# The pooling stage of a two-layer encoder: scale folded into the map's weights, gate row finished earlier, boundary work reordered

## The chip, the cores and the metric

The kernel runs on one core of one Trainium2 chip. The metric is the time of one execution in microseconds (us), as the median of several runs. The core's engines run side by side, each through its own queue in order: TensorE (PE, its weight loads are PEld), VectorE (DVE), ScalarE (ACT), GpSimd (POOL), and SyncE (SP), which issues the loads from memory.

## The reference

The input is 256 tokens of 1024 channels. Two layers follow each other, each made of three sublayers: a SwiGLU with 2816 hidden channels, a token mixer, and a second SwiGLU. The mixer of layer 0 is a pooling mixer, that of layer 1 latent attention. Every sublayer is wrapped in the same way, with shift, scale and gate computed from a conditioning vector `c`:

```
h = rmsnorm(x, g_pre) * (1 + scale) + shift
y = rmsnorm(fn(h), g_post)
x = x + weight * (1 + gate) * y
```

The pooling mixer works in four groups of 256 channels. Group g takes the mean over a window of 2, 4, 8 or 16 tokens minus the token itself, multiplies by its 256x256 map, adds a bias and multiplies by a scale for every channel:

```
y = einsum('bsgc,gcd->bsgd', pooled - hg, w) + b
return y.reshape(B, S, D_MODEL) * scale
```

## The kernel before, in words

The 256 tokens are two token tiles of 128. A sublayer's input `h` lies turned (channels on partitions) as two float32r parts, hTH (the rounded value) and hTL (the rest), and every weight likewise: ACT casts a raw tile to the high part (line 263), VectorE subtracts it from the raw tile for the low part (line 271). A product is three matmuls, high by high, high by low, low by high (lines 98 to 100).

**Order of the work.** The program is recorded in the order in which the code calls it (no scheduler moves anything), so each engine runs its share in that order. The class `Bulk` holds one queue of all loads of the program: four raw buffers of 1 MB (`N_RAW`), each load followed by its ACT work and its VectorE work. A load is issued by SP when a raw buffer is free again, so VectorE's progress sets when loads start. `until`, `high`, `low_part` and `soft` let the stages run pieces of this queue at chosen places.

**A SwiGLU** (class `FFN`; f0 and f2 are those of layer 0) runs over 11 chunks of 256 hidden channels. `unit` does one chunk of one token tile: product with `wi`, silu and gate product `g` (lines 708, 710), transposes of `g` (724) with its split gH, gL (94, 95), product with `wo` into four accumulator banks (747). `head` does chunks 0 and 1 while tile 1's boundary work (`chain1`) is still under way; `tail` does chunks 9 and 10, tile 0 ahead of tile 1, so that tile 0's boundary is covered by tile 1's products.

**A boundary** from one sublayer to the next is a chain across engines, per token tile: sums of squares of y on ACT (508), `ms` on VectorE (501), the power on POOL (503), x += y * G * r on VectorE (535), sums of squares of x (ACT), `ms`, POOL, xr = x * r in halves on ACT and VectorE (554, 555), transposes on TensorE (562), modulation in halves on ACT and VectorE (576, 582), cast to hTH (588, 590) and hTL (593).

**Modulation vectors** take four 1 MB pieces of `ada_w` each (tiles `ada`), summed on VectorE over the conditioning channels into `aacc` (350, 352); TensorE then sums over partitions, either by eight matmuls of one column (361, `finish_cols`), by transposes that VectorE adds up (391 and 397, `finish_turned`), or, for a gate, into a row G on all partitions (448, then 456 and 457 add the bias and multiply by (1 + gate) g_post).

**The pooling stage** follows f0's tail. Tokens are mixed after the map, by a 256x256 matrix for each group. `pool_map` multiplies h of one tile by the map's parts pwH, pwL into z; ACT copies z out (1461, 1476, 1477); `pool_bias` starts an accumulator bank with the bias (954); `pool_mix` adds the mixed z (965); `pool_scale_rows` multiplies by the scale on VectorE into `pooly` (979), from which the boundary reads. The gate row of the pooling sublayer is reduced in the stage itself (448, 456, 457), and so are shift and scale of the next sublayer, vectors 6 and 7 (361). `warm` matmuls (108) keep TensorE occupied near the stage's end.

## Time and profile before

| | |
|---|---|
| median of 3 runs (lowest to highest) | 930.23 us (930.08 to 932.29) |
| profiled execution, span from first to last instruction | 928.2 us |
| its own time, with what lies around the span | not listed apart; 930.2 by the median of the runs, 2.0 beyond the span |
| TensorE busy | 902.1 us (97%) |
| TensorE weight loads | 741.1 us (80%) |
| VectorE busy | 705.8 us (76%) |
| ScalarE busy | 441.1 us (48%) |
| GpSimd busy | 41.9 us (5%) |
| read from memory | 233.51 MB, 253 GB/s over the span |

A timeline row reads: start in us from the span's first instruction, duration in us, engine, line of the kernel, operation, output <- inputs, shapes, how many instructions the row merges, and in brackets how long the engine had stood idle before it and what ended that. A windows row gives a stretch, its length, then for PE, PEld, DVE, ACT and POOL the busy time and the number of instructions, then the granted TensorE clock (1.00 is full), the DMA engines' busy share and the GB/s moved.

### The profile page before, as it was taken

What the parts mean: (1) busy time and instruction counts of PE and PEld (TensorE: products, weight loads), DVE (VectorE), ACT (ScalarE), POOL (GpSimd) and SP (SyncE); (2) the same over time, 40 slices, a digit from 0 to 9 for tenths busy, and PEclk for the clock granted to TensorE, in tenths of its full rate; (3) what the DMA queues carried; (4) which work ended last, traced back from release to release, by engine and by line L of the source; (5) the groups of instructions that cost most, each with busy time, mean ns of one, the idle gap of its engine ahead of it and who ended that gap; (6) DMA issues with size and microseconds to landing.
All of it is one profiled execution on the core that took longest, in us unless ns stands there. A gap on an engine that the chain in (4) does not pass through costs nothing.

```text
span 928.2 us, 11193 instructions
## 1 busy us (share of the span) xinstructions
PE 902.1 (97%) x4251; PEld 741.1 (80%) x4251; DVE 705.8 (76%) x856; ACT 441.1 (48%) x661; POOL 41.9 (5%) x56
## 2 busy tenths in 40 slices
...
GB/s 324 370 313 352 364 372 311 345 373 210 137 181 287 376 342 323 303 365 268 137 203 371 320 350 322 346 234 32 53 130 100 173 156 278 292 194 259 226 1 45
DMA packets 135973, 235.28 MB, mean 253 GB/s; under 512 B 5628, under 2 KB 98415, under 8 KB 135664
## 3 DMA queue, kind: packets, MB, share of 16 engines
...
q14 instruction: 20, 0.16, 0.0%
HBM read 233.51 MB, written 1.05 MB: 253 GB/s over the span
## 4 chain that ended last, share of the span: by engine, by line
PE 89%; DVE 4%; ACT 3%; issue 2%; DMA 1%; POOL 0%; SPq 0%; DVEq 0%; POOLq 0%; ACTq 0%
PE acc L747 25%; PE in L100 16%; PE in L98 16%; PE in L99 16%; PE accm L1314 2%; PE ps_g L724 2%; PE ps_h L562 1%; PE ps_mod L361 1%; DVE aacc L352 1%; PE in L794 1%; PE accp L965 1%; DMA adah<-in_ada_w_dram 1%; ACT p L1228 1%; DMA wi<-in_ffn_w_in_dram 1%; PE ps_turn L391 1%
## 5 line engine op out<-in xcount | busy, mean ns | idle before, releaser
L352 DVE SCALAR_TENSOR_TENSOR aacc<-ada,sc,aacc 128x1024 f32<-128x1024 f32 (+1 forms) x113 | 143.8, 1273 | 11.3 <-DMA ada<-in_ada_w_dram 9.1
L708 ACT ACTIVATE sil<-in 128x256 f32<-128x256 f32 x84 | 32.2, 383 | 247.7 <-PE in L100 240.4
L710 DVE TENSOR_TENSOR g<-in,sil 128x256 f32<-128x256 f32 x84 | 35.2, 420 | 52.4 <-ACT sil L708 52.3
L95 DVE TENSOR_TENSOR gL<-ps_g,gH 128x256 fp32r<-128x256 f32 x88 | 36.7, 417 | 23.6 <-ACT gH L94 23.5
L94 ACT CAST gH<-ps_g 128x256 fp32r<-128x256 f32 x88 | 32.4, 368 | 45.1 <-PE ps_g L724 45.0
L503 POOL TENSOR_TENSOR r<-ms,mhalf 128x1 f32<-128x1 f32 x24 | 13.6, 565 | 838.4 <-DVE ms L501 838.4
L724 PEld LDWEIGHTS ps_g<-ident,g 128*128 128x128 f32 x176 | 24.7, 140 | 11.5
L724 PE MATMUL ps_g<-ident,g 128*128 128x128 f32 x176 | 33.6, 272 | 0.0
L508 ACT ACTIVATE junk<-x 128x512 bf16<-128x512 f32 x24 | 15.1, 631 | 21.4 <-DVE x L535 11.3
L361 PE MATMUL ps_mod<-ones,aacc 128*128 128x1 f32 x96 | 12.7, 259 | 10.1 <-DVE cols L150 9.9
L576 ACT ACTIVATE hs<-ps_h,mod,mod 128x128 f32<-128x128 f32 x48 | 18.1, 458 | 8.4 <-DVE mod L377 5.0
L361 PEld LDWEIGHTS ps_mod<-ones,aacc 128*128 128x128 f32 x96 | 13.0, 210 | 11.2 <-DVE cols L150 10.1
L352 DVE SCALAR_TENSOR_TENSOR aacc<-adah,sc,aacc 128x512 f32<-128x512 f32 x28 | 21.0, 752 | 0.9
L582 DVE TENSOR_SCALAR hs<-ps_h,mod,mod 128x128 f32<-128x128 f32 x48 | 16.4, 404 | 5.2 <-PE ps_h L562 4.9
L535 DVE SCALAR_TENSOR_TENSOR x<-tmp,r,x 128x512 f32<-128x512 f32 x23 | 16.3, 749 | 2.2 <-POOL r L503 1.2
L1238 POOL TENSOR_SCALAR p<-p,rs 128x256 f32<-128x256 f32 x16 | 16.1, 1008 | 28.6 <-ACT p L1228 15.3
L554 ACT ACTIVATE xr<-x,r 128x512 f32<-128x512 f32 x12 | 8.7, 722 | 17.4 <-POOL r L503 17.4
L1228 ACT ACTIVATE p<-s,nm 128x256 f32<-128x256 f32 x32 | 14.9, 471 | 3.1 <-DVE nm L1220 2.6
L593 DVE TENSOR_TENSOR hTL<-hs,hTH 128x512 fp32r<-128x512 f32 x24 | 15.6, 688 | 0.4
L562 PE MATMUL ps_h<-ident,xr 128*128 128x128 f32 x96 | 14.3, 292 | 0.5 <-ACT xr L554 0.3
L271 DVE TENSOR_TENSOR wo10L<-wo,wo10H 128x2048 fp32r<-128x2048 f32 x4 | 9.2, 2293 | 7.4 <-ACT wo10H L263 7.4
L1263 PE MATMUL att<-pT,v 128*128 128x256 f32 x52 | 13.8, 389 | 0.5 <-ACT pT L1255 0.3
...
## 6 DMA issues: line engine op xcount, KB each, us to landing
...
```

The lines of the kernel that those rows point to most:

```text
L94: nc.scalar.copy(h, src)
L95: nc.vector.tensor_sub(lo, src, h.bitcast(F32))
L98: nc.tensor.matmul(ps, lhsT=lh, rhs=rh, start=first, stop=False)
L99: nc.tensor.matmul(ps, lhsT=lh, rhs=rl, start=False, stop=False)
L100: nc.tensor.matmul(ps, lhsT=ll, rhs=rh, start=False, stop=last)
L352: nc.vector.scalar_tensor_tensor(acc, w, sc[:, k : k + 1], acc, op0=ALU.mult, op1=ALU.add)
L361: nc.tensor.matmul(ps[:, j : j + 1], lhsT=acc[:, (j - j0) * P : (j - j0 + 1) * P], rhs=ones[:, 0:1], start=True, stop=True,)
L708: nc.scalar.activation(sil, ps[:, 0:CW], AF.Silu)
L710: nc.vector.tensor_mul(g, ps[:, CW : 2 * CW], sil)
L724: nc.tensor.transpose(ps[:, a * P : (a + 1) * P], g[:, a * P : (a + 1) * P], ident)
L747: nc.tensor.matmul(acc[hf], lhsT=lhs[:, a, :], rhs=rhs[:, a, hf * 512 : (hf + 1) * 512], start=f, stop=l)
L1228: nc.scalar.activation(p[:, t * S : (t + 1) * S], ps[:, t * S : (t + 1) * S], AF.Exp, bias=nm[:, t : t + 1], accum_out=sm[:, t : t + 1],)
```

## The change

1. The pooling scale is multiplied into the raw map `pw` on VectorE (`pool_scaled`, two halves) before it is split, and into the bias row (one partition, 1024 elements). The accumulator then holds the scaled result, and `pool_scale_rows` and `pooly` go.
2. The map, the scale row and the bias row are loaded earlier, together with the second of the four pieces of vector 7 (`with_pool`); until the map has been split, the queue of loads keeps three raw buffers instead of four (`limit`).
3. The gate row of the pooling sublayer is finished in f0's last chunks, in the place of its own sum `aacc` (`in_place`). Vector 6 is no longer held for the stage: it is turned in f0's body (`finish_turned`).
4. In the stage the boundary chain comes first on every engine: ACT's copies of z, the bias and mixing matmuls and the low parts of f2's first weights come after the chain's steps. The halves of xr and of the modulation change engines (`act_half`, `own`): the half that VectorE scales is also cast by VectorE.
5. f2's first low parts are cut into halves or quarters (`low_part`) and put at chosen places; all of wi01L and wi10L now stands behind the boundary's last VectorE instruction.
6. Matmuls on the low part hTL come last in `pool_map` and in the first half of chunk 0 in `head` (`low_last`; in f2, f3 and f5). Most `warm` matmuls go.

```diff
@@ class Bulk @@
+            self.limit = N_RAW
...
-                if out >= N_RAW:
+                if out >= self.limit:
@@ gate(..., in_place=False) @@
-                if hf == 0:
+                if hf == 0 and in_place:
+                    mods[layer, m] = acc
+                    st.append(acc)
+                elif hf == 0:
                     st.append(row_tile())
@@ mod_half(..., own=False) @@
-            if on_act:
+            if on_act != own:
                 nc.vector.tensor_copy(hh[:, bsl, :], hv)
@@ FFN.mm_in(..., low_last=False) @@
+            if low_last:
+                todo = [(hh, i, k) for k in ks for i in range(2)] + [(hl, 0, k) for k in ks]
...
@@ pooling mixer @@
+    def pool_load():
+        raw = raw_tile("pw")
+        nc.sync.dma_start(
+            raw.rearrange("p (k n) -> p k n", n=GW), pool_w[0].rearrange("g (a p) n -> p (g a) n", p=P)
+        )
+        sr = rowp.tile([P, D], F32, tag="xr", name="poolsc")
+        nc.sync.dma_start(sr, pool_scale[0:1, :].to_broadcast([P, D]))
+        br = rowp.tile([P, D], F32, tag="xr", name="poolb")
+        nc.sync.dma_start(br[0:1, :], pool_b[0:1].rearrange("l g n -> l (g n)"))
+        pool_st.update(raw=raw, sr=sr, br=br)
...
+    def pool_scaled(hf):
+        rv = pool_st["raw"][:, hf * 1024 : (hf + 1) * 1024].rearrange("p (g a n) -> p g a n", g=2, a=2)
+        sv = pool_st["sr"][:, hf * 512 : (hf + 1) * 512].rearrange("p (g n) -> p g n", g=2)
+        nc.vector.tensor_mul(rv, rv, sv.unsqueeze(2).to_broadcast([P, 2, 2, GW]))
...
-        nc.sync.dma_start(bs[0:1, 0:D], pool_b[0:1].rearrange("l g n -> l (g n)"))
-        nc.sync.dma_start(bs[:, D : 2 * D], pool_scale[0:1, :].to_broadcast([P, D]))
+        nc.vector.tensor_mul(bs[0:1, 0:D], pool_st["br"][0:1, :], pool_st["sr"][0:1, :])
@@ the program's loads @@
-    ss2 = shift_scale(0, 2, (6, 7))
+    ss2 = shift_scale(0, 2, (7,))
+    def with_pool():
+        bulk.limit = N_RAW - 1
+        pool_load()
+        ss2[5][1]()
+
+    early = (ss2[5][0], with_pool, *ss2[5][2:])
...
     def to_pool():
-        bulk.until(("pw",))
+        for hf in range(2):
+            a = hf * 1024
+            pool_scaled(hf)
+            bulk.high_part(("pw",), a, a + 1024)
+        bulk.low_part(("pw",), 0, 1024, False)
+        bulk.limit = N_RAW
+        bulk.low_part(("pw",), 1024, 2048, True)
+        pool_consts()
@@ layer 0, pooling (now) @@
+    s2 = post_add(1, acc1, r, mods[0, 2])
+    nc.scalar.copy(*z0[1])
...
+    xr = pre_scale(1, rstd(s2, 1.0), 1)
...
+    pool_mix(accp0, 0, 0)
...
+    pool_mix(accp0, 0, 1)
+    accp1 = acc_tile(1, "accp1")
+    pool_bias(1, accp1, 0)
+    after = reduce_held(0, 7, psum.tile([P, 512], F32, tag="in", name="ps_mod07"))
+    pool_bias(1, accp1, 1)
+    pool_mix(accp1, 1, 0)
+    G = mods[0, 5]
+    r = post_norm(0, accp0, 1.0, G)
...
+    h0()
+    h1()
+    l0()
+    l1()
+    bulk.low_part(wi(0, 1), 0, 1024, False)
+    bulk.low_part(wi(0, 1), 1024, 2048, True)
+    f2.high_in(1, 0)
+    bulk.low_part(wi(1, 0), 0, 1024, False)
+    bulk.low_part(wi(1, 0), 1024, 2048, True)
```

The first place where instructions move is VectorE's queue in f0's last chunks, between the last pieces of vector 7 and the boundary of tile 0 (`gL` is the low part of a turned chunk, `tmp` the boundary's first product). Before:

```order
L352 SCALAR_TENSOR_TENSOR aacc_1514<-ada_1454,sc,aacc_1514 128x1024 x2
L271 TENSOR_TENSOR wo10L<-wo_1458,wo10H 128x2048
L95 TENSOR_TENSOR gL_1582<-ps_g_1578,gH_1581 128x256
L710 TENSOR_TENSOR g_1587<-in_1542,sil_1585 128x256
L271 TENSOR_TENSOR pwL<-pw,pwH 128x2048
L95 TENSOR_TENSOR gL_1624<-ps_g_1620,gH_1623 128x256
L523 TENSOR_TENSOR tmp_1652<-acc_0_492,G_1145 128x512
```

The same place now:

```order
L457 TENSOR_TENSOR aacc_1327<-ps_row_1558,bc 128x512
L458 SCALAR_TENSOR_TENSOR aacc_1327<-aacc_1327,bc 128x512
L353 SCALAR_TENSOR_TENSOR aacc_1532<-ada_1474,sc,aacc_1532 128x1024 x2
L272 TENSOR_TENSOR wo10L<-wo_1505,wo10H 128x2048
L95 TENSOR_TENSOR gL_1601<-ps_g_1597,gH_1600 128x256
L721 TENSOR_TENSOR g_1606<-in_1562,sil_1604 128x256
L457 TENSOR_TENSOR aacc_1327<-ps_row_1608,bc 128x512
L458 SCALAR_TENSOR_TENSOR aacc_1327<-aacc_1327,bc 128x512
L944 TENSOR_TENSOR pw<-pw,poolsc 128x1024 x2
L272 TENSOR_TENSOR pwL<-pw,pwH 128x1024 x2
L950 TENSOR_TENSOR poolbs<-poolb,poolsc 1x1024
L95 TENSOR_TENSOR gL_1658<-ps_g_1654,gH_1657 128x256
```

Four gate instructions, two products with the scale row and the bias product now stand ahead of `gL` and so of the whole boundary of tile 0.

The second place is SP's queue of loads in the same chunks (`wo` is the last chunk's output weight, used by TensorE ahead of everything in the stage). Before:

```order
L291 DMA ada_1448<-in_ada_w_dram 128x2x1024
L291 DMA ada_1454<-in_ada_w_dram 128x2x1024
L657 DMA wo_1458<-in_ffn_w_out_dram 128x2x1024
L914 DMA pw<-in_pool_w_dram 128x8x256
L291 DMA ada_1517<-in_ada_w_dram 128x2x1024
```

The same place now:

```order
L292 DMA ada_1462<-in_ada_w_dram 128x2x1024
L923 DMA pw<-in_pool_w_dram 128x8x256
L927 DMA poolsc<-in_pool_scale_dram 128x1024
L929 DMA poolb<-in_pool_b_dram 1x1024
L292 DMA ada_1474<-in_ada_w_dram 128x2x1024
L662 DMA wo_1505<-in_ffn_w_out_dram 128x2x1024
L292 DMA ada_1589<-in_ada_w_dram 128x2x1024
```

The map (1 MB) and the scale row on all partitions (0.5 MB) moved ahead of the last `wo`.

The third place is VectorE's queue where f2 begins (`hTH` and `hTL` are f2's input for tile 0, `tmp` begins the boundary of tile 1). Before:

```order
L588 CAST hTH_1979<-hs_1986 128x512
L593 TENSOR_TENSOR hTL_1980<-hs_1986,hTH_1979 128x512
L593 TENSOR_TENSOR hTL_1980<-hs_1996,hTH_1979 128x512
L271 TENSOR_TENSOR wi10L<-wi_1704,wi10H 128x2048
L523 TENSOR_TENSOR tmp_2041<-pooly,G_1800 128x512
L501 SCALAR_TENSOR_TENSOR ms<-ss 128x1
L526 TENSOR_TENSOR tmp_2041<-pooly,G_1800 128x512
L535 SCALAR_TENSOR_TENSOR x_81<-tmp_2041,r,x_81 128x512 x2
L271 TENSOR_TENSOR wi11L<-wi_1882,wi11H 128x2048
```

The same place now:

```order
L593 CAST hTH_1964<-hs_1971 128x512
L598 TENSOR_TENSOR hTL_1965<-hs_1971,hTH_1964 128x512
L598 TENSOR_TENSOR hTL_1965<-hs_1981,hTH_1964 128x512
L272 TENSOR_TENSOR wi01L<-wi_1647,wi01H 128x1024 x2
L272 TENSOR_TENSOR wi10L<-wi_1733,wi10H 128x1024 x2
L527 TENSOR_TENSOR tmp_2034<-accp_0_1909,aacc_1327 128x512
L505 SCALAR_TENSOR_TENSOR ms<-ss 128x1
L530 TENSOR_TENSOR tmp_2034<-accp_1_1910,aacc_1327 128x512
L539 SCALAR_TENSOR_TENSOR x_81<-tmp_2034,r,x_81 128x512 x2
L272 TENSOR_TENSOR wi11L<-wi_1900,wi11H 128x2048
```

The low part wi01L, which was made ahead of the boundary of tile 0, now stands between f2's input and everything else.

## Rows read from the trace of the kernel before

**Rows 1.** Windows: the last chunks of f0, the pooling stage, f2's head.
```profile
204.00:211.00 7.00, 7.00 (x35) 5.75 (x33) 5.03 (x4) 2.45 (x3) 0.00 (x0) 1.00 0.98 360
...
222.87:252.89 30.02, 29.39 (x171) 24.01 (x169) 24.34 (x44) 19.74 (x39) 2.20 (x4) 0.94 0.37 130
252.89:264.74 11.85, 11.85 (x50) 9.05 (x51) 10.68 (x14) 6.33 (x9) 1.41 (x2) 1.00 0.44 131
264.74:300.00 35.26, 35.26 (x164) 29.23 (x164) 25.41 (x28) 17.19 (x22) 0.00 (x0) 1.00 0.74 246
```

**Rows 2.** Timeline of f0's last two chunks: ScalarE, VectorE and TensorE.
```profile
201.84 1.91 ACT L263 CAST wo10H<-wo 128x2048 fp32r<-128x2048 f32 x1 [4.29 <-DMA wo<-in_ffn_w_out_dram]
203.78 2.29 DVE L271 TENSOR_TENSOR wo10L<-wo,wo10H 128x2048 fp32r<-128x2048 f32 x1
...
211.62 0.42 DVE L95 TENSOR_TENSOR gL<-ps_g,gH 128x256 fp32r<-128x256 f32 x1 [1.30 <-ACT gH L94]
217.10 0.42 DVE L710 TENSOR_TENSOR g<-in,sil 128x256 f32<-128x256 f32 x1 [0.73 <-ACT sil L708]
217.62 0.38 PEld L724 LDWEIGHTS ps_g<-ident,g 128*128 128x128 f32 x2
...
222.87 0.19 PEld L98 LDWEIGHTS z<-pwH,hTH 128*128 128x128 f32 x1
```

**Rows 3.** Timeline of TensorE in f0's body, around four transposes and a gate's half row.
```profile
121.19 0.60 PE L391 MATMUL ps_turn<-ident,aacc 128*128 128x128 f32 x4
...
121.86 0.40 PE L99 MATMUL in<-wi50L,hTH 128*128 128x512 f32 x1
...
156.69 1.02 PE L448 MATMUL ps_row<-aacc,ones 128*128 128x512 f32 x2
...
157.78 0.40 PE L99 MATMUL in<-wi70L,hTH 128*128 128x512 f32 x1
```

**Rows 4.** One line of the gate row, and a half low part in the timeline.
```profile
L456 DVE TENSOR_TENSOR G<-ps_row,bc x10: 680/692/692, 148.5 to 882.7; 128x512 f32<-128x512 f32 x10
...
261.95 1.22 DVE L271 TENSOR_TENSOR wo0L<-wo,wo0H 128x1024 fp32r<-128x1024 f32 x1
```

**Rows 5.** Timeline of the pooling stage: the chain's places, both token tiles.
```profile
224.90 1.41 DVE L535 SCALAR_TENSOR_TENSOR x<-tmp,r,x 128x512 f32<-128x512 f32 x2
...
226.16 0.59 ACT L1461 COPY poolz<-z 128x512 f32<-128x512 f32 x1 [0.85 <-PE z L100]
...
229.17 0.72 ACT L554 ACTIVATE xr<-x,r 128x512 f32<-128x512 f32 x1 [1.05 <-POOL r L503]
...
231.59 1.04 PE L562 MATMUL ps_h<-ident,xr 128*128 128x128 f32 x8
...
234.47 0.19 PEld L98 LDWEIGHTS z<-pwH,hTH 128*128 128x128 f32 x1 [0.76 <-DVE hTH L588]
...
241.22 1.28 DVE L979 TENSOR_TENSOR pooly<-accp,poolbs 128x512 f32<-128x512 f32 x2
...
243.50 0.16 DVE L501 SCALAR_TENSOR_TENSOR ms<-ss 128x1 f32<-128x1 f32 x1 [0.41 <-ACT junk L508]
...
248.21 0.72 ACT L554 ACTIVATE xr<-x,r 128x512 f32<-128x512 f32 x1 [0.85 <-POOL r L503]
```

**Rows 6.** The clock near the stage's end: two windows, and twelve equal weight loads twice.
```profile
247.00:248.00 1.00, 1.00 (x6) 1.00 (x6) 0.30 (x2) 0.36 (x2) 0.37 (x1) 0.50 0.13 53
...
250.00:251.00 1.00, 1.00 (x10) 1.00 (x9) 0.00 (x0) 0.60 (x3) 0.00 (x0) 0.84 0.00 0
...
247.03 2.68 PEld L108 LDWEIGHTS warm<-ident 128*128 128x128 f32 x12
...
250.82 1.42 PEld L108 LDWEIGHTS warm<-ident 128*128 128x128 f32 x12
```

**Rows 7.** Timeline of f2's head: low part of chunk 1 and the end of tile 1's boundary.
```profile
261.75 0.19 PEld L99 LDWEIGHTS in<-wi11L,hTH 128*128 128x128 f32 x1 [0.34 <-DVE wi11L L271]
...
264.74 0.86 PEld L562 LDWEIGHTS ps_h<-ident,xr 128*128 128x128 f32 x8 [0.22 <-ACT xr L554]
```

More of the change, by code (lines that the diff above doesn't have):

```diff
@@ L550, in pre_xr, with pre_scale @@
         return pre_scale(t, rstd(s2, 1.0))
-    def pre_scale(t, r):
+    def pre_scale(t, r, act_half=0):
         xr = rowp.tile([P, D], F32, tag="xr", name=f"xr{t}")
-        nc.scalar.activation(xr[:, 0:512], xt[t][:, 0:512], AF.Copy, scale=r)
-        nc.vector.tensor_scalar(xr[:, 512:1024], xt[t][:, 512:1024], r, None, op0=ALU.mult)
+        a, v = (slice(hf * 512, (hf + 1) * 512) for hf in (act_half, 1 - act_half))
+        nc.scalar.activation(xr[:, a], xt[t][:, a], AF.Copy, scale=r)
+        nc.vector.tensor_scalar(xr[:, v], xt[t][:, v], r, None, op0=ALU.mult)
         return xr
@@ L698, in need_out, with mm_in @@
             bulk.until(("wo", self.layer, self.fi, c))
-        def mm_in(self, ps, c, t, hT, ks):
+        def mm_in(self, ps, c, t, hT, ks, low_last=False):
             hh, hl = hT
+            if low_last:
+                todo = [(hh, i, k) for k in ks for i in range(2)] + [(hl, 0, k) for k in ks]
+                for n, (lhs, i, k) in enumerate(todo):
+                    rhs = self.wi[c, k // 4][i][:, k % 4, :]
+                    nc.tensor.matmul(ps, lhsT=lhs[:, k, :], rhs=rhs, start=n == 0 and k == 0, stop=False)
+                return
             for k in ks:
@@ L711, in act, with inn @@
             self.st[c, t] = g
-        def inn(self, c, t, hT, mid=nop):
+        def inn(self, c, t, hT, mid=nop, low_last=False):
             ps = psum.tile([P, 512], F32, tag="in", name=f"in{c}{t}")
-            self.mm_in(ps, c, t, hT, range(4))
+            self.mm_in(ps, c, t, hT, range(4), low_last)
             mid()
@@ L754, in head @@
             self.need_in(0, 1)
-            ps = self.inn(0, 0, hT0)
+            ps = self.inn(0, 0, hT0, low_last=True)
             self.need_in(1, 0)
@@ L971, in pool_mix @@
             )
-    def pool_scale_rows(t, acc, halves=(0, 1)):
-        if "y" not in pool_st:
-            pool_st["y"] = hl_tile("pooly", F32)
-        y = pool_st["y"][:, t * D : (t + 1) * D]
-        for hf in halves:
-            sl = slice(hf * 512, (hf + 1) * 512)
-            nc.vector.tensor_mul(y[:, sl], acc[hf], pool_st["bs"][:, D + hf * 512 : D + (hf + 1) * 512])
-        return [y[:, 0:512], y[:, 512:1024]]
     mla = {}
@@ L1450 @@
     hT0 = ffn_tail(
         f0, hT, 0, 0, 0, 1, to_pool,
-        between=lambda: bulk.low_part(ada2, 0, 1, False),
-        between2=(lambda: bulk.low_part(ada2, 1, 2, False, 0, 512), last_ada2),
+        between=first_ada2,
+        between2=(lambda: bulk.low_part(ada2, 1, 2, False, 0, 512), lambda: bulk.low_part(ada2, 1, 2, True, 512, D)),
     )
     acc1 = f0.acc[1]
-    z0 = pool_map(0, hT0)
+    wi = lambda c, q: ("wi", 0, 1, c, q)
+    z0 = [pool_map(0, hT0, hf) for hf in range(2)]
     r = post_norm(1, acc1, 0.5, mods[0, 2])
-    for dst, src in z0:
-        nc.scalar.copy(dst, src)
@@ L1462 @@
-    s2 = post_add(1, acc1, r, mods[0, 2])
-    rows_of_gate = held["pool"]([psum.tile([P, 512], F32, tag="in", name=f"ps_row{hf}") for hf in range(2)])
-    rows_of_gate([0])
-    accp0 = pool_bias(0)
-    pool_mix(accp0, 0, 0)
-    xr = pre_xr(1, s2)
-    rows_of_gate([1])
-    bulk.low_part(ada3, 0, 1, False)
-    f2.high_in(0, 0)
-    hT1 = pre(1, xr, 0, 1)
-    accp1 = pool_bias(1)
-    (dst0, src0), (dst1, src1) = pool_map(1, hT1)
-    bulk.low_part(ada3, 1, 2, True)
-    f2.high_in(0, 1)
@@ L1493 @@
-    xr = pre_xr(0, s2)
-    pool_scale_rows(1, accp1, (1,))
-    ss = post_sq(y1, 1.0)
-    for f in after:
-        f()
-    hT0 = pre(0, xr, 0, 2)
-    more(6)
+    nc.scalar.copy(*z0[0])
+    s2 = post_add(1, acc1, r, mods[0, 2])
+    nc.scalar.copy(*z0[1])
+    accp0 = acc_tile(0, "accp0")
+    for hf in range(2):
+        pool_bias(0, accp0, hf)
+    xr = pre_scale(1, rstd(s2, 1.0), 1)
+    hT1 = new_hT(1)
+    h0, l0, _ = mod_half(1, 0, turn_half(1, 0, xr), hT1, 0, 1, False, True)
+    h1, l1, _ = mod_half(1, 1, turn_half(1, 1, xr), hT1, 0, 1, True, True)
@@ new lines @@
+    h0()
+    h1()
+    pool_mix(accp0, 0, 0)
+    l0()
+    bulk.low_part(ada3, 0, 1, False)
+    l1()
+    f2.high_in(0, 0)
+    z1 = [pool_map(1, hT1, hf) for hf in range(2)]
+    for dst, src in z1:
+        nc.scalar.copy(dst, src)
+    bulk.low_part(ada3, 1, 2, True)
+    bulk.low_part(wi(0, 0), 0, 1024, False)
+    pool_mix(accp0, 0, 1)
[3 more added lines that the diff above has]
+    pool_bias(1, accp1, 1)
```

98 lines of the change are left out of this document (43 added, 55 removed).

## The prediction

> **What bounds the kernel now.** I read the busy times by window first. TensorE is busy all the time in f0's last chunks, in f2's head and after it, and its clock is full there [rows 1]. So each matmul added to those stretches costs its own time, and whatever makes TensorE wait in the pooling stage is never made up later. The stage takes 30.0 us, most of it for waits along the boundary chains of the two token tiles. Second I read the timeline of f0's last chunks: VectorE works at 5.0 of 7.0 us there, idle mostly for ScalarE's casts (1.30 before gL), and the last `wo` comes late from memory (ScalarE idle 4.29 us for it) [rows 1, 2]. Third the timeline of the stage, for the places of the chain [rows 5], and fourth f2's head, where TensorE already waits 0.34 us for the low part wi11L and 0.22 us for the boundary of tile 1 [rows 7]: VectorE has no slack left there.
>
> The profiled span is 928.2 us and the median 930.2, so I put 2.0 us around the span and make the sum on 930.2.
>
> **First stretch, f0's body and tail.** TensorE gets eight transposes for vector 6, in two groups of four. From the start of such a group to the second matmul behind it are 0.67 us, where one matmul alone takes 0.23: 0.44 us each. The gate's half row costs 1.09 - 0.23 = 0.86 us [rows 3]. Together 2 x 0.44 + 2 x 0.86 = 2.6 us, all on the path, since TensorE has no gap here.
>
> VectorE gets more, and what decides is when it reaches `g` of the last chunk, for which TensorE comes at 217.62 before [rows 2] and at 220.2 with the 2.6 us. The last `wo` landed at 201.8 [rows 2]; 1.57 MB (map and scale row) now stand ahead of it in the queue, at 360 GB/s [rows 1] 4.3 us, so about 206. Bounds of that delay: none, if the loads have room, and 5.2 us if they run at 300 GB/s; I take 4.2, since the DMA engines are busy at 0.98 of the window [rows 1]. Then in order: cast to wo10H 1.9 (207.9), wo10L 2.3 (210.2), gL and g of the chunk before 0.7 (210.9), the gate's second half 2 x 0.69 (212.3) [rows 2, 4]. No row shows a product with a repeated row; the nearest, 1024 elements of a tile by a tile, took 1.22 [rows 4], and 2.29 is the bound if it ran at half the rate: 2 x 1.2 (214.6). The map's low part in halves 2 x 1.22 instead of 2.29 (217.1). The bias product runs on one partition, which no row shows: between the 0.16 us of a one-element instruction [rows 5] and the 1.22 of 1024 elements [rows 4]; I take 1.2, as it has as many elements along a partition (218.3). The Trainium skill, "VectorE: DVE Perf Modes" (The TRN2 errata), gives (N + 151) / 0.96 ns for a float32 product of N elements per partition, 1.22 us here whatever the number of partitions; by it the sum would be the same. Then gL at 218.3 where it was at 211.62, and from gL to the end of g the work between (boundary products, x, a 1.3 us step of vector 7) takes 4.8 us: 5.9 before, less 1.1 of idle time in it, 0.73 of that in front of g [rows 2]. So g is there at 223.1. TensorE stands 2.9 us at 220.2. So z starts 5.5 us later than at 222.87 (2.6 if VectorE were in time, 6.5 with the slow loads).
>
> **Second stretch, the pooling stage**, on the old clock with z at 222.87 [rows 5]. ScalarE's copy of z at 226.16 no longer stands between tile 1's x (first half ready some 0.75 us after 224.90) and its sums, nor the gate's half row on VectorE: xr 1.1 us earlier, at 228.1. Tile 1's transposes no longer wait behind the mixing of tile 0: 231.59 becomes 228.7, and z of tile 1 starts at 231.05 instead of 234.47 (0.5 us more than at the transposes, since VectorE has no step of vector 7 in front of its modulation). z of tile 1 ends at 234.2; wi00H now stands ahead of its copies on ScalarE, so tile 0's accumulator is whole at 235.8, but its first half is there at 235.5, where VectorE began its scale product only at 241.22 (behind wi01L and two matmuls of the other tile). Without that product (0.6 us for the half that counts) `ms` is at 236.9 instead of 243.50. Without tile 1's scale product between x and `ms`, xr is at 240.9 instead of 248.21. But TensorE is then still at the bias rows (2 x 0.86), the eight one-column sums (2.0) and six mixing matmuls (2.5) and comes to the transposes at 242.1. Modulation 1.4 and cast 0.4 on VectorE as before, and f2 starts at 244.7 instead of 252.89, with 0.4 us more for the small gaps that released instructions show: 7.8 us gained (8.2 without the gaps, 6.5 if wi00H or the two last mixing matmuls come out late). The clock is part of it: from 247 it stood at 0.50, that is 1.2 GHz, right after the sixteen one-column sums, and twelve weight loads took 2.68 instead of 1.42 us [rows 6]; half of these sums are gone from the stage.
>
> **Third stretch, f2's head.** VectorE makes wi01L here (2 x 1.2), which was done before the stage's end, and hTL waits for ScalarE's cast of the second half (0.3): wi11L is ready 2.7 us later against f2's start, and none of it is hidden, since TensorE waited for it already [rows 7]. ps_h of tile 1 stands 14.5 us behind f2's start instead of 11.85: 2.65 us given back (1.3 if half of wi01L fits into VectorE's waits for POOL, 3.2 if the load of wi11 is late too). After it TensorE is busy throughout [rows 1], and I let the rest stand: in f3's and f5's heads I found no wait of TensorE for hTL, so `low_last` brings nothing there.
>
> **Sum:** 930.2 + 5.5 - 7.8 + 2.65 = 930.6 us. The stage is shorter by a quarter, and nearly all of that goes to TensorE's added work and VectorE's queue before and behind it.
>
> **The rivals.**
> - *VectorE is in time (faster).* If the last `wo` is not held up by the map's load, its queue ends 2.7 us earlier and TensorE meets no wait at `g`; if the low parts in the head also cost only the lower bound: 930.2 + 2.6 - 7.8 + 1.3 = 926.3. For it: DMA share falls to 0.37 in the stage [rows 1], so the loads have slack somewhere. Against: ScalarE did wait 4.29 us for just this load [rows 2].
> - *The clock falls (slower).* TensorE now stands 2.9 us at `g` and 2.7 us at wi11L. Before, its clock fell after the one-column sums and was at 0.50 from 247 to past 250, some 3.3 us [rows 6]. If it falls so behind both waits, each costs half of that: 930.6 + 3.3 = 933.9; one fall alone (932.3) doesn't decide. Against: waits of 0.2 to 0.8 us left the clock full [rows 1, 5, 7]. The Trainium skill, "TensorE: Matmul & The Clock Gate" (Why this matters for your kernels), tells one to leave no longer idle gaps between bursts of matmuls, since the clock goes back to its lower level; by that rule this rival would be the forecast. No row of before shows so long a wait behind dense matmuls, so I give it less.
> - *The loads set f2's pace.* Then what the stage gains or loses is made up or lost later, and the time stays at 930.2. Against: TensorE is busy 35.26 of 35.26 us behind the head [rows 1].
>
> **How the numbers follow.** Forecast 0.58, VectorE in time 0.20, clock 0.17, loads 0.05. About 0.3% (2.8 us, 927.4 and 933.0) is what a measurement can tell from no change. The forecast and the loads lie within it but for some 0.02 on either edge, and the first rival below it, the second above: faster 0.21, same 0.61, slower 0.18. The range reaches from 927.2 to 934.0: the bounds of the three stretches alone (2.6 to 6.5, 8.2 to 6.5, 1.3 to 3.2) give 925.9 to 933.4, and the clock reaches a little further; I leave out the far ends of the first two rivals.
>
> **What would show it.** Right: wo10H on ScalarE near 206, TensorE waiting 2 to 4 us at ps_g for `g` before z, the stage from z to f2's first matmul 22 to 23 us, TensorE waiting 2 to 3 us at wi11L, full clock in all of it, and equal distances after f2's chunk 2. Wrong: no wait at `g` (then the first stretch is 2.6), a stretch at 0.50 behind a wait, a stage of 25 us or more (then a step on VectorE or ScalarE that I put beside the chain is on it), or time lost or won after the head.

## The result: slower by 0.5%

The changed kernel takes 934.4 us (median of 13 runs, 931.38 to 937.26), the kernel before 929.73 in the same runs: a ratio of 1.0051 (95% interval 1.0039 to 1.0063). The forecast was 930.6 with a range up to 934.0, so it was wrong, and on the slow side. The profiled execution of the changed kernel took 935.7 us, 1.8 beyond its span. Its page:

```profile
span 933.9 us, 11142 instructions
...
PE 900.4 (96%) x4221; PEld 736.9 (79%) x4221; DVE 708.2 (76%) x862; ACT 440.7 (47%) x663; POOL 41.6 (4%) x56
...
PEclk9999999999799999999999999999999999999999
```

TensorE is busy for 1.7 us less than before, and yet the program is longer: it waits more, and in one slice (the eleventh, 233.5 to 256.8) its clock is visibly down. The windows, with the columns of [rows 1], of the three stretches of the forecast and of three places inside them:

```profile
224.00:227.00 3.00, 3.00 (x8) 2.32 (x9) 2.14 (x5) 0.98 (x2) 0.55 (x1) 0.51 0.43 175
230.67:258.02 27.35, 26.75 (x128) 20.47 (x126) 17.46 (x36) 16.18 (x34) 2.20 (x4) 0.81 0.27 88
238.00:241.00 3.00, 3.00 (x10) 2.47 (x9) 2.93 (x6) 2.97 (x6) 0.00 (x0) 0.50 0.03 5
248.50:254.50 6.00, 6.00 (x13) 3.76 (x14) 2.27 (x7) 2.72 (x6) 0.55 (x1) 0.50 0.26 69
258.02:271.98 13.96, 11.64 (x50) 9.13 (x50) 13.03 (x17) 9.76 (x14) 1.10 (x2) 1.00 0.58 186
271.98:307.00 35.02, 35.02 (x163) 29.04 (x163) 24.77 (x27) 16.42 (x21) 0.00 (x0) 1.00 0.73 244
```

Against [rows 1]: z starts at 230.67 instead of 222.87 (7.8 us later, forecast 5.5); the stage takes 27.35 instead of 30.02 us (2.7 won, forecast 7.8); the head takes 13.96 instead of 11.85 (2.1 lost, forecast 2.65); behind it TensorE is busy throughout in both. The stage ran at a mean of 0.81 where before it was 0.94, with TensorE busy in all but 0.6 us of it.

Now the places. The timeline of f0's end, ScalarE, VectorE and TensorE (before: [rows 2]):

```profile
207.27 1.90 ACT L264 CAST wo10H<-wo 128x2048 fp32r<-128x2048 f32 x1 [9.32 <-DMA wo<-in_ffn_w_out_dram]
...
211.54 0.19 PEld L758 LDWEIGHTS acc<-wo10L,gH 128*128 128x128 f32 x1 [1.31 <-DVE wo10L L272]
...
213.40 2.35 DVE L944 TENSOR_TENSOR pw<-pw,poolsc 128x1024 f32<-128x1024 f32 x2
...
218.02 1.21 DVE L950 TENSOR_TENSOR poolbs<-poolb,poolsc 1x1024 f32<-1x1024 f32 x1
219.15 0.41 DVE L95 TENSOR_TENSOR gL<-ps_g,gH 128x256 fp32r<-128x256 f32 x1
...
223.51 0.42 DVE L721 TENSOR_TENSOR g<-in,sil 128x256 f32<-128x256 f32 x1
...
223.99 0.65 PE L735 MATMUL ps_g<-ident,g 128*128 128x128 f32 x2 [2.46 <-DVE g L721]
...
226.15 1.05 PE L758 MATMUL acc<-wo9H,gL 128*128 128x512 f32 x2
```

SyncE's issue of the last wo, before and now, and what the issue waited for now:

```profile
195.84 0.37 SPq L657 DMA_DIRECT2D wo<-in_ffn_w_out_dram  x1
...
199.60 0.37 SPq L662 DMA_DIRECT2D wo<-in_ffn_w_out_dram  x1
...
SPq L662 <- DVE wo9L L272: 2.4, 1, 2.4
```

The last wo came at 207.3 (forecast 206). It was issued 3.8 us later than before, because the map now takes a raw buffer ahead of it and the wo has to wait for one release more, that by wo9L; and it came 7.7 us behind its issue instead of 6.0. The two products with the scale row took 1.22 each and the bias product 1.21 (1.2 each), gL began at 219.15 (218.3), g ended at 223.9 (223.1). TensorE waited 1.31 us for wo10L, which the forecast did not have, and 2.46 for g (2.9). By the starts of the same work on TensorE in both traces it was 0.5 us ahead before the added matmuls (in the trace of before the clock fell once near 25 us, in this one it did not) and 2.2 behind after them, so they cost 2.7 (2.6); then it fell back by 1.3 at wo10L, 2.6 at g, and 1.7 more, because behind the wait the clock was at 0.51: two matmuls of 512 columns took 1.05 us there instead of 0.62.

The stage, TensorE and the chain of tile 0 (before: [rows 5, 6]):

```profile
233.85 1.98 PE L969 MATMUL accp<-poolbs,ones 1*128 1x512 f32 x4
236.42 1.09 PE L567 MATMUL ps_h<-ident,xr 128*128 128x128 f32 x8 [0.59 <-DVE xr L560]
237.35 3.25 PE L979 MATMUL accp<-poolz,mix 128*128 128x256 f32 x8
...
245.49 1.12 PE L969 MATMUL accp<-poolbs,ones 1*128 1x512 f32 x2
246.54 2.22 PEld L362 LDWEIGHTS ps_mod<-ones,aacc 128*128 128x128 f32 x16 [0.76 <-issue]
...
248.77 2.07 PE L969 MATMUL accp<-poolbs,ones 1*128 1x512 f32 x2
...
250.58 0.72 ACT L559 ACTIVATE xr<-x,r 128x512 f32<-128x512 f32 x1 [0.99 <-POOL r L507]
...
250.77 4.83 PE L979 MATMUL accp<-poolz,mix 128*128 128x256 f32 x12
255.44 1.04 PE L567 MATMUL ps_h<-ident,xr 128*128 128x128 f32 x8
```

The chain did shorten: xr of tile 0 came 19.9 us behind z where it was 25.3 (forecast 18.0). But TensorE reached its transposes only at 24.8 behind z (forecast 19.2). The second bias row and the mixing matmuls in front of them stood at 0.50 (windows 238.00 and 248.50; the lower level lasted 3.4 us behind 237.5 and 6.8 behind 247.8): the second bias row took 2.07 us where the same had taken 1.12, and the mixing 4.83.

f2's head, VectorE and TensorE (before: [rows 7]):

```profile
259.31 2.35 DVE L272 TENSOR_TENSOR wi01L<-wi,wi01H 128x1024 fp32r<-128x1024 f32 x2
261.58 2.35 DVE L272 TENSOR_TENSOR wi10L<-wi,wi10H 128x1024 fp32r<-128x1024 f32 x2
...
266.66 2.28 DVE L272 TENSOR_TENSOR wi11L<-wi,wi11H 128x2048 fp32r<-128x2048 f32 x1
...
268.99 0.19 PEld L99 LDWEIGHTS in<-wi11L,hTH 128*128 128x128 f32 x1 [2.71 <-DVE wi11L L272]
```

VectorE makes wi01L behind f2's input and is then late at wi11L, for which TensorE's weight loads wait 2.71 us where they had waited 0.34. Its clock stayed at 1.00 here.

### The profile page after: what moved, and what is told of

It is laid out like the page before. It is cut to its first block, busy times and chain, and to the rows that moved or that the text cites. A ratio compares the mean times of both kernels' runs of the same rounds, so it can differ in the third digit from the quotient of the medians.

```text
span 933.9 us, 11142 instructions
## 1 busy us (share of the span) xinstructions
PE 900.4 (96%) x4221; PEld 736.9 (79%) x4221; DVE 708.2 (76%) x862; ACT 440.7 (47%) x663; POOL 41.6 (4%) x56
## 3 DMA queue, kind: packets, MB, share of 16 engines
HBM read 233.51 MB, written 1.05 MB: 251 GB/s over the span
## 4 chain that ended last, share of the span: by engine, by line
PE 81%; DVE 9%; ACT 3%; DMA 3%; issue 3%; POOL 1%; SPq 0%; DVEq 0%; POOLq 0%; ACTq 0%
PE acc L758 24%; PE in L100 14%; PE in L99 14%; PE in L98 14%; PE accm L1319 2%; DVE aacc L353 2%; PE ps_g L735 2%; DMA wo<-in_ffn_w_out_dram 2%; DMA wi<-in_ffn_w_in_dram 1%; PE ps_h L567 1%; PE accp L979 1%; PE ps_mod L362 1%; PE ps_turn L392 1%; PE in L711 1%; ACT p L1233 1%
## 5 line engine op out<-in xcount | busy, mean ns | idle before, releaser
L353 DVE SCALAR_TENSOR_TENSOR aacc<-ada,sc,aacc 128x1024 f32<-128x1024 f32 (+1 forms) x113 | 143.8, 1272 | 13.9 <-DMA ada<-in_ada_w_dram 11.7
L95 DVE TENSOR_TENSOR gL<-ps_g,gH 128x256 fp32r<-128x256 f32 x88 | 36.6, 416 | 22.3 <-ACT gH L94 22.2
L735 PEld LDWEIGHTS ps_g<-ident,g 128*128 128x128 f32 x176 | 24.6, 140 | 14.4 <-DVE g L721 3.2
L362 PEld LDWEIGHTS ps_mod<-ones,aacc 128*128 128x128 f32 x80 | 10.8, 211 | 13.5 <-DVE cols L150 10.1
L1233 ACT ACTIVATE p<-s,nm 128x256 f32<-128x256 f32 x32 | 14.9, 470 | 3.2 <-DVE nm L1225 2.7
L398 DVE TENSOR_REDUCE mod<-ps_turn 128x4 f32<-128x512 f32 x14 | 9.5, 685 | 8.5 <-PE ps_turn L392 8.5
## 6 DMA issues: line engine op xcount, KB each, us to landing
adah<-in_ada_w_dram SPq DMA_DIRECT2D x4, 512.0 KB, 11.7
```

The costliest lines, as they stand in the source:

```text
L95: nc.vector.tensor_sub(lo, src, h.bitcast(F32))
L353: nc.vector.scalar_tensor_tensor(acc, w, sc[:, k : k + 1], acc, op0=ALU.mult, op1=ALU.add)
L362: nc.tensor.matmul(ps[:, j : j + 1], lhsT=acc[:, (j - j0) * P : (j - j0 + 1) * P], rhs=ones[:, 0:1], start=True, stop=True,)
L735: nc.tensor.transpose(ps[:, a * P : (a + 1) * P], g[:, a * P : (a + 1) * P], ident)
L1233: nc.scalar.activation(p[:, t * S : (t + 1) * S], ps[:, t * S : (t + 1) * S], AF.Exp, bias=nm[:, t : t + 1], accum_out=sm[:, t : t + 1],)
```

## The experiments

The granted clock of every run is listed beside its time. So each kernel's time can be split: 2 x (1 - mean clock) x span is the time that the run spent at the lower level, and half of it is what the clock cost at most (some 2 to 4 us of it lie behind TensorE's last matmul, where they cost nothing). Each ratio is to the runs of the kernel before beside it. The last two columns are means over the runs of a kernel. The first of them has a standard error of 0.5 us for before and of about 1 for the others; the second repeats better: for the kernel before it lay between 922.0 and 922.6 beside each of the five sets of experiments.

| kernel | median, us | ratio to before (interval) | at the lower clock, us | time less half of that |
|---|---|---|---|---|
| before (108 runs) | 929.8 | 1 | 14.6 | 922.3 |
| changed | 934.4 | 1.0051 (1.0039 to 1.0063) | 19.2 | 924.6 |
| e1: wi01L ahead of f2's input | 931.5 | 1.0020 (1.0002 to 1.0038) | 15.4 | 923.7 |
| e2: map loaded behind the last wo | 930.7 | 1.0012 (0.9995 to 1.0029) | 18.3 | 921.1 |
| e3: vector 7 turned | 931.4 | 1.0023 (1.0007 to 1.0039) | 14.9 | 923.9 |
| e4: matmuls in the wait at g | 935.1 | 1.0055 (1.0038 to 1.0073) | 20.8 | 924.2 |
| e5: e1, e2, e3, GpSimd helps | 927.9 | 0.9974 (0.9962 to 0.9987) | 12.8 | 921.1 |
| e6: bias rows over 128 partitions | 930.8 | 1.0012 (0.9998 to 1.0026) | 14.1 | 923.7 |
| e7: e2, e6, weights split earlier | 924.1 | 0.9954 (0.9935 to 0.9972) | 9.6 | 919.4 |
| e8: e6's edit on the kernel before | 928.0 | 0.9987 (0.9973 to 1.0001) | 12.2 | 921.8 |
| e9: e7 without e6's edit | 928.1 | 0.9972 (0.9951 to 0.9993) | 16.2 | 919.8 |
| e10: e7 again | 923.7 | 0.9925 (0.9911 to 0.9939) | 8.3 | 919.6 |
| e11: e9 again | 927.7 | 0.9976 (0.9961 to 0.9990) | 14.4 | 920.5 |
| e12: changed again | 935.3 | 1.0044 (1.0029 to 1.0059) | 20.2 | 924.9 |

The first two rows hold the verdict: of the 4.7 us between the means (934.2 and 929.6), 2.3 are work and waits at full clock, and 2.3 are the clock.

**Where the clock fell.** In windows of 1 us over the whole span, every fall of every trace, up to the last matmul, lasts 3.4 us or twice that, and the pooling stage is not the only place. Two more in the trace of before:

```profile
25.00:29.00 4.00, 4.00 (x6) 1.54 (x5) 3.86 (x8) 2.71 (x3) 0.00 (x0) 0.57 1.07 377
...
642.00:650.00 8.00, 8.00 (x34) 7.37 (x35) 4.65 (x12) 4.69 (x8) 0.23 (x1) 0.57 0.01 2
```

TensorE is busy throughout in both; the second begins within sixteen more one-column sums, in layer 1. No edit touches these two places, and from trace to trace the lower level lasts 0, 3.4 or 6.8 us in each of them. So a stage's loss is read in its own window, and the mean over runs holds the other places too. The changed kernel's trace is 7.2 us behind the one of before at f2's chunk 2 (7.8 - 2.7 + 2.1), and 5.7 at the end: near 650 us its clock was low for 3.4 us, where the one of before lost 6.8.

**The theory** after the result: three losses that add up, the late load with VectorE's queue behind it, f2's head, and the lower clock in the stage. **Rivals:** the order on VectorE alone, with a clock that only happened to be low; or losses that overlap, so that mending one brings out the next.

**Run e1.**

```
     bulk.high_part(wi(0, 1), 1024, 2048)
+    bulk.low_part(wi(0, 1), 0, 1024, False)
+    bulk.low_part(wi(0, 1), 1024, 2048, True)
     hT0 = new_hT(0)
...
-    bulk.low_part(wi(0, 1), 0, 1024, False)
-    bulk.low_part(wi(0, 1), 1024, 2048, True)
     f2.high_in(1, 0)
```

> One edit on the changed kernel: both halves of the low part wi01L are made ahead of f2's input on VectorE, in the 4.41 us in which VectorE stands before the modulation of tile 0, instead of behind that input. Theory (order on VectorE): TensorE's 2.29 us wait at wi11L falls to under 0.5, ps_h of tile 1 stands 11.9 to 12.2 us behind f2's first matmul instead of 13.96, and the time falls by 2 us, to about 932.4 (ratio to the kernel before 1.003). Rival (the loads or GpSimd's power set f2's head): the wait stays over 1.5 us and the time within 0.7 us of 934.4. Second rival: wi01L comes so late out of ScalarE's cast that it delays the modulation; then the stage grows by what the head wins.

The median fell by 2.9 us, but only 0.9 of it at full clock. Its timeline of the head, VectorE and TensorE:

```profile
254.92 2.36 DVE L272 TENSOR_TENSOR wi10L<-wi,wi10H 128x1024 fp32r<-128x1024 f32 x2 [1.12 <-ACT wi10H L264]
...
262.35 0.19 PEld L99 LDWEIGHTS in<-wi11L,hTH 128*128 128x128 f32 x1 [1.64 <-DVE wi11L L272]
```

The head took 12.90 us, half of the 2.1 came back. The other half has another cause: the changed kernel also casts wi10 to wi10H behind f2's input, and VectorE now waits 1.12 us for that cast. So neither theory was quite right: order, but on two engines (e7 below moves both).

**Run e2.**

```
-    early = (ss2[5][0], with_pool, *ss2[5][2:])
...
+        def load():
+            pool_load()
+            st.append(pool_st["raw"])
+
+        bulk.add(("pw",), load, *split_work("pw", st, put))
```

> One edit on the changed kernel: map, scale row and bias row are loaded behind f0's last wo again, and the pieces of vector 7 by the ordinary rule of four buffers. Theory (the load delays wo10, and VectorE's queue behind it sets the wait at g): the cast to wo10H starts near 203 instead of 207.3, the 0.89 us wait at wo10L goes, the wait at ps_g falls from 2.46 to under 0.7 us and with it the fall of the clock at 224 (0.50 for 3.4 us, 1.7 us lost); z starts 4 to 5 us earlier, near 226, and the time is 929.5 to 930.5 (ratio 1.000 to 1.001). Rival (VectorE's added work alone sets it): wo10 earlier, but the scale product now waits for the map, so g stays late and the time gains under 1.5 us.

Its timeline of f0's end, and its windows of stage and head:

```profile
202.14 1.91 ACT L264 CAST wo10H<-wo 128x2048 fp32r<-128x2048 f32 x1 [3.58 <-DMA wo<-in_ffn_w_out_dram]
...
220.62 0.38 PE L735 MATMUL ps_g<-ident,g 128*128 128x128 f32 x2
```

```profile
225.61:251.42 25.81, 25.19 (x128) 19.76 (x126) 17.50 (x36) 16.23 (x34) 2.19 (x4) 0.87 0.34 109
251.42:266.72 15.30, 12.99 (x49) 10.27 (x50) 13.89 (x17) 9.75 (x14) 1.09 (x2) 0.89 0.62 203
```

The edit takes `with_pool` and its limit of three buffers out as well. The wo is issued at 196.1 again, the cast begins 5.1 us earlier, both waits are gone, and z starts at 225.61, 5.1 us earlier: VectorE's added products cost nothing once the load is in time. At full clock the runs gain 3.5 us (924.6 to 921.1); the time, 930.7, is just above the range expected. The clock fell elsewhere instead: in the head, behind the wait at wi11L, 15.30 us at 0.89 where the changed kernel took 13.96 at 1.00.

**Runs e3 and e4** look for what brings the clock down.

```
-    after = reduce_held(0, 7, psum.tile([P, 512], F32, tag="in", name="ps_mod07"))
+    after = [f() for f in held.pop((0, 7))]
```

> One edit on the changed kernel: vector 7 is turned by eight transposes and added up on VectorE instead of summed by eight one-column matmuls in the stage. Theory (one-column sums bring the clock down): no stretch at 0.50 between the sums and f2's first matmul; the stage falls from 27.35 to 23.5 to 24.5 us, the time to 931 to 931.8 (ratio 1.0015 to 1.002). Rival (the clock falls for the short waits and the one-partition bias rows around them): the 0.50 stays within 2 us of where it was, the stage is 26 us or more and the time within 1.2 us of 934.4.

```
             def mid():
+                if self.fi == 0 and self.layer == 0:
+                    warm(8, "in", 2)
                 self.tr(c10, 1)
```

> One edit on the changed kernel: eight matmuls whose result nobody reads are put on TensorE where it waits 2.46 us for g of the last chunk. Theory (that wait brings the clock down): no 0.50 behind the wait, the 13 matmuls there take 1.6 us less, z starts 1.3 to 1.7 us earlier and the time is about 932.8 (ratio 1.0033). Rival (the wait is harmless and the fall came from something before it): the clock falls at the same place, and the time stays at 934.4 or grows by what the eight matmuls take over the wait.

Windows of e3 (stage, and the place of the sums), then of e4 (behind the wait at g, and head), and the wait at g in e6, the next run:

```profile
231.14:255.28 24.14, 22.78 (x121) 17.41 (x119) 18.62 (x38) 16.15 (x34) 2.19 (x4) 0.93 0.19 59
...
248.00:255.00 7.00, 6.22 (x32) 4.70 (x32) 6.02 (x15) 4.28 (x10) 0.55 (x1) 1.00 0.07 7
```

```profile
224.00:229.22 5.22, 5.22 (x28) 4.29 (x29) 4.43 (x11) 3.40 (x8) 0.55 (x1) 1.00 0.52 167
...
255.03:270.34 15.31, 12.98 (x49) 10.23 (x50) 13.88 (x17) 9.76 (x14) 1.10 (x2) 0.89 0.62 206
```

```profile
223.38 0.44 PE L735 MATMUL ps_g<-ident,g 128*128 128x128 f32 x2 [2.50 <-DVE g L721]
```

Without the sums the fall behind them is gone (1.00 from 248 to 255), and the runs spend 4.3 us less at the lower clock; the one behind the first bias rows stayed. In e4 there was no fall at g, as expected, and z came 1.45 us earlier; but there was a new one behind wi11L, and the time was 935.1 instead of the 932.8 expected. Nor does e4 show that the wait brings the fall: e6 waits for g as long as the changed kernel (2.50 us), and its clock is at 1.00 from there to z. The Trainium skill, "TensorE: Matmul & The Clock Gate" (Why this matters for your kernels), asks for no long idle gaps between matmul bursts. The falls behind the two waits may be of that kind, but the same waits came without one: at g the weight loads waited 2.7 to 2.9 us in the changed kernel, e3 and e12 with a fall and in e6 without, at wi11L 2.7 to 2.8 us in e2 and e4 with one and in the changed kernel, e3 and e6 without. In the stage, where the engine was busy and the clock fell all the same, that sentence says nothing.

**Run e6**, therefore, tests the other thin work in the stage, the bias rows.

```
+        pool_st["bs"] = hl_tile("poolbs", F32)
+        nc.gpsimd.memset(pool_st["bs"][:, 0:D], 0.0)
...
-            lhsT=ones[0:1, :],
-            rhs=pool_st["bs"][0:1, hf * 512 : (hf + 1) * 512],
+            lhsT=ones,
+            rhs=pool_st["bs"][:, hf * 512 : (hf + 1) * 512],
```

> One edit on the changed kernel: the bias rows are added by matmuls over 128 partitions (127 of them zeros, laid down by GpSimd) instead of over one; same count and shape otherwise. Theory that matmuls with little in them bring the clock down, one-partition ones as well as one-column ones: the 0.50 at 237.7, behind the first four bias rows, goes, the time at the lower clock falls from a mean of 19.2 us per run to 15 or less, and the time to 932 to 932.5. Rival (only the one-column sums and the waits do): as much time at 0.50 as before the edit, and the time within 1 us of 934.4.

Windows of its stage and head, and the same places of TensorE's timeline:

```profile
228.62:250.66 22.04, 21.12 (x128) 17.47 (x126) 17.47 (x36) 16.12 (x34) 2.20 (x4) 1.00 0.31 98
250.66:264.64 13.98, 11.65 (x50) 9.13 (x51) 13.04 (x17) 9.75 (x15) 1.10 (x2) 1.00 0.70 240
```

```profile
242.84 1.84 PE L362 MATMUL ps_mod<-ones,aacc 128*128 128x1 f32 x16
244.54 1.10 PE L969 MATMUL accp<-poolbs,ones 128*128 128x512 f32 x2
245.49 2.75 PE L979 MATMUL accp<-poolz,mix 128*128 128x256 f32 x12
```

The stage takes 22.04 us at full clock, against the 22.2 of the forecast, with the one-column sums still in it. Matmuls over 128 partitions cost no more than those over one (1.10 and 1.12 us a row), and the 0.76 us that TensorE's weight loads had stood ahead of the sums for nothing visible are 0.24. The theory stands for the stage; the rival would have left the 0.50 there. The runs spend 5.1 us less at the lower clock, and the time is 930.8 where 932 to 932.5 was expected. The trace gained more than the stage: the fall at g is missing in it as well, though the bias rows run behind it, and what took that one away no run shows.

**Run e5** put e1 to e3 together, and gave GpSimd the second halves of wi01L and wi10L.

```
+    bulk.low_part(wi(0, 1), 0, 1024, False)
     bulk.high_part(wi(0, 1), 1024, 2048)
+    bulk.low_part(wi(0, 1), 1024, 1536, False, nc.gpsimd)
+    bulk.low_part(wi(0, 1), 1536, 2048, True, nc.gpsimd)
+    bulk.high_part(wi(1, 0), 0, 1024)
...
+    bulk.low_part(wi(1, 0), 1024, 1536, False, nc.gpsimd)
+    bulk.low_part(wi(1, 0), 1536, 2048, True, nc.gpsimd)
```

> The changed kernel with the edits of three runs before (map loaded behind the last wo, vector 7 turned, wi01L ahead of f2's input), and two more for f2's head: the second half of wi01L and of wi10L is made on GpSimd (1.29 us for 512 elements in the trace of before), and ScalarE casts the first half of wi10 ahead of the modulation. Theory (the three losses are separate: load and queue 3.5 us, sums 1 us and the clock behind them 2 us, head 2 us): z near 225.6, the stage 22 to 23.5 us, the wait at wi11L under 0.5 and the head 11.6 to 12.2 us; the time 925 to 927, faster than the kernel before (ratio 0.995 to 0.998). Rival (the losses overlap: without one wait the next is as long, or GpSimd's low parts slow VectorE or delay the power of a boundary): head over 13 us or stage over 25 us at full clock, the time 929 to 931.

Its timeline around f2's start, GpSimd and VectorE:

```profile
247.57 2.84 POOL L272 TENSOR_TENSOR wi01L<-wi,wi01H 128x512 fp32r<-128x512 f32 x2 [1.77 <-PE ps_h L567]
...
249.38 1.32 DVE L593 CAST hTH<-hs 128x512 fp32r<-128x512 f32 x1
...
251.94 2.31 DVE L272 TENSOR_TENSOR wi10L<-wi,wi10H 128x1024 fp32r<-128x1024 f32 x1
```

It beats the kernel before, by less than expected (927.9 for 925 to 927): the head is 12.07 us, but the stage 25.91, with TensorE waiting 1.7 us for f2's input. Beside GpSimd's work VectorE's cast took 1.32 us instead of 0.43, and half a low part 2.31 instead of 1.22. The Trainium skill, "GPSIMD Engine Reference" (8. Key points), says that GpSimd shares its memory interfaces with VectorE, and names VectorE's instructions with two inputs, and those in a mode that takes two ports, as the ones that collide. The low part (two inputs) agrees; whether the cast, which slowed threefold, is of the second kind no run shows.

**Run e7** does without GpSimd: e2 and e6 together, wi00H cast in f0's tail, wi00L in quarters in VectorE's waits, most of wi01L and all of wi10H in the stage.

```
-    xr = pre_scale(1, rstd(s2, 1.0), 1)
+    bulk.low_part(wi(0, 0), 0, 512, False)
+    rr = rstd(s2, 1.0)
+    bulk.low_part(wi(0, 0), 512, 1024, False)
+    xr = pre_scale(1, rr, 1)
+    bulk.low_part(wi(0, 0), 1024, 1536, False)
...
+    bulk.high_part(wi(1, 0), 1024, 2048)
     hT0 = new_hT(0)
...
-    bulk.low_part(wi(0, 1), 0, 1024, False)
-    bulk.low_part(wi(0, 1), 1024, 2048, True)
-    f2.high_in(1, 0)
+    bulk.low_part(wi(0, 1), 1536, 2048, True)
```

> The changed kernel with the map loaded behind the last wo and the bias rows over 128 partitions, and f2's first weights split earlier without GpSimd: ScalarE casts wi00 in f0's tail, wi01 and wi10 in the stage; VectorE makes wi00L in quarters (0.69 us) in its waits of the first boundary, three quarters of wi01L in the stage and the last behind f2's input. Vector 7 keeps its one-column sums. Theory (the losses are separate, and add up): z near 225.6, the stage near 22.0 us at full clock as with the bias rows alone, the wait at wi11L under 1 us and the head 11.9 to 12.5 us, the time 923.5 to 925.5 (ratio 0.994 to 0.996), at the lower clock 14 us per run or less. Rival (the quarters stand in the chain, or the clock falls for the sums once TensorE waits less): the stage 24 us or more, the time 927 or more.

Its windows of stage and head:

```profile
224.82:247.17 22.35, 21.12 (x128) 17.48 (x126) 19.34 (x40) 16.10 (x34) 2.51 (x4) 1.00 0.37 126
247.17:259.46 12.29, 11.65 (x50) 9.13 (x50) 11.37 (x16) 7.95 (x13) 1.09 (x2) 1.00 0.65 214
```

Every part came out as expected: z at 224.8, the stage 22.35, the head 12.29, the time 924.1. It is the fastest kernel here: 0.46% below the kernel before (interval 0.28 to 0.65%), and 0.75% when it ran again (e10, below). At full clock it is 5.2 us below the changed kernel, where e2 (3.5), e6 (1.0) and the shorter head (1.7) make 6.2: the losses nearly add up, and do not hide each other.

**Runs e8 to e12** ask whether the 128 partitions did it. e8 makes e6's edit on the kernel before; e9 takes it out of e7. e7 and e9 ran on different chips, so e10, e11 and e12 are e7, e9 and the changed kernel on one.

> One edit on the kernel before: its bias rows are added over 128 partitions (127 of zeros) instead of one. If the one-partition matmuls bring the clock down there too: no 0.50 between z and f2's first matmul, the time at the lower clock falls from a mean of 14.3 us per run to under 12, the stage from 30.0 to 28 us, and the time by 1 to 2 us (ratio 0.998 to 0.999). Rival (in the kernel before the fall belongs to its sixteen one-column sums, which come long behind the bias rows): the fall at 247 stays, and the time is the same within 0.7 us.

> The best kernel so far (map behind the last wo, first weights of f2 split earlier, bias rows over 128 partitions) with the bias rows over one partition again, and no other edit. If the one-partition matmuls bring the clock down: one or two stretches at 0.50 in the stage, the time at the lower clock rises from a mean of 9.6 us per run to 13 or more, the stage to over 24 us, and the time from 924.1 to 926.5 to 928 (ratio 0.997 to 0.9985). Rival (what the 128 partitions won in the changed kernel was another position of the falls by chance): time at the lower clock within 2 us of 9.6, and the time within 1.2 us of 924.1.

> The kernel of run e7 once more, on the same chip as e11 and e12, since e7 and e9 ran on two chips. If the bias rows over 128 partitions keep the clock up: at the lower clock 9 to 12 us per run in the mean, 4 us or more below e11; at full clock the same as e11 within 0.6 us. Rival (chance of the chips): within 2 us of e11.

> The kernel of run e9 once more (bias rows over one partition), beside e10. If the one-partition matmuls bring the clock down: at the lower clock 14 to 17 us per run, the time 2 to 3.5 us above e10. Rival: within 1 us of e10.

> The changed kernel itself once more, beside e10 and e11. By the sum of the parts: at full clock 2.2 to 2.6 us above the kernel before and 5.2 above e10, at the lower clock 18 to 20 us per run, the time 4.5 to 5 us above the kernel before and 9 to 10 above e10. Rival (the clock's share of the loss was chance): at the lower clock as much as the kernel before within 2 us, the time 2 to 3 us above it.

A window of e8 behind its sixteen sums, and the stages of e10, e11 and e12:

```profile
249.00:251.00 2.00, 1.85 (x10) 1.58 (x9) 1.10 (x5) 1.77 (x5) 0.00 (x0) 0.50 0.01 4
```

```profile
225.74:248.12 22.38, 21.12 (x128) 17.47 (x126) 19.37 (x40) 16.14 (x34) 2.51 (x4) 1.00 0.37 129
```

```profile
225.47:250.13 24.66, 23.68 (x128) 18.42 (x126) 19.35 (x40) 16.13 (x34) 2.58 (x4) 0.93 0.34 117
```

```profile
230.30:257.69 27.39, 26.76 (x128) 20.51 (x126) 17.51 (x36) 16.23 (x34) 2.19 (x4) 0.81 0.27 90
```

On one chip the pair agrees with e6: with one partition instead of 128 the time at the lower clock rises by 6.1 us (e7 to e9: 6.6) and the median by 4.0, in intervals that do not touch, while at full clock the two differ by 1.0 and 0.4 us. Of the 6.1 the trace of e11 shows one fall of 3.4 us in the stage; where the runs have the rest no trace shows. e12 repeats the changed kernel's stage to 0.04 us, with the clock at 0.81 again. Over all traces with the new order of the stage, the nine with one-partition bias rows have a fall in it (3.4 us in e1, e3, e5, e9 and e11, 6.8 in e2 and e4, 10.2 in the changed kernel and e12), and the three with 128 partitions (e6, e7, e10) have none, which is hard to put down to chance. Some forecasts of size missed: the gap between e10 and e11 (4.0 us) was expected at 2 to 3.5, their difference at full clock (1.0) within 0.6, and e12's 935.3 lies 11.7 above e10 where 9 to 10 was expected. In e8 the rival holds for the place: the fall behind the sixteen sums stays. Its time is 1.6 us lower, with an interval that touches 1, so whether the kernel before gains by the edit is left open.

## Why the prediction was wrong, step by step

- **First stretch, +5.5: right in what waits for what, a little small.** VectorE's queue came out as listed, each product within 0.02 us, and the added matmuls cost 2.7 (2.6). The load was 1.3 us later than I took (207.3 against 206), 5.4 us later than before and so just beyond the bound of 5.2 for slow loads. That the size came near is partly luck: I counted bytes ahead of the wo, and 3.8 of the 5.4 us are its later issue, one raw buffer later behind the map. At full clock the stretch lost 2.7 + 1.3 + 2.6 = 6.6. e2 shows that the map's place is the cause: with the load in time only the added matmuls are left.
- **Second stretch, -7.8: this step failed**, at "from 247 it stood at 0.50 ... half of these sums are gone from the stage", which counted on full clock from z to f2. At full clock the forecast holds: 22.2 against 22.04 in e6 and 22.35 in e7. In the changed kernel the stage ran at 0.81, that is 10.2 us at the lower level, 5.1 us lost where before 3.4 us cost 1.7. In the forecast's own terms, the bias rows, sums and six mixing matmuls in front of the transposes (2 x 0.86 + 2.0 + 2.5 = 6.2) took 9.95 us, from 245.49 to 255.44, and 6.1 in e6; the earlier fall, behind 237.5, cost the other 1.7. The forecast looked at the sixteen one-column sums alone, and overlooked the one-partition bias rows, of which the new order put one on either side of the eight sums that are left: from 245.5 to 250.8 TensorE did nothing but these three. The trace of before already had falls with TensorE busy at 25 and 642 us, which the forecast did not read.
- **Third stretch, +2.65: right**, 2.1 by a wait of 2.71 us of the weight loads at wi11L. The reason was half of it: e1 shows that wi10H's cast on ScalarE, also moved behind f2's input, is the other half.
- **The sum.** Without the 1.7 us that the clock cost the stage before, the forecast was 5.5 - 6.1 + 2.65 = 2.05 us slower; the two traces give 6.6 - 6.1 + 2.1 = 2.6, the runs 2.3 at full clock. What is missing is the clock: 4.6 us more at the lower level per run, 2.3 us.
- **The rivals.** "The clock falls" came nearest in time (933.9) and was given 0.17, but by luck. Its two places were the waits; the fall at g came, the one at wi11L only in e2 and e4, and the larger part lay in the stage, where the rival had none. "VectorE is in time" would have been right with the load where it was: e2. "The loads set f2's pace" fell: nearly all that e5 and e7 had won at f2's start (2.1 and 5.7 us, by the start of the same weight load) was still there behind its head (1.9 and 5.3).
